# A hybrid attention step on one core: output projection 512 columns wide, sample rows in column tiles of TensorE, and a stricter model behind the order

## The chip, the cores and the metric

One core of one Trainium2 chip runs the whole program. The metric is the device time of one execution in microseconds (us), as the median of several runs. The engines are named as in the profile: PE is TensorE's matmul side, PEld its weight loads, DVE is VectorE, ACT is ScalarE, POOL is GpSimd, SP issues the DMAs.

## The reference, cut to what matters

One layer with three head groups works on 512 prompt rows and 32 sample rows of width 1024. Everything is float32.

```
z = rmsnorm(x) @ w_in                              # q, k, v, gate of A, B, M and the indexer's qi, ki, wi
A: 6 heads x 64, chunk-band attention (own chunk + 8 before), learned relative bias
B: 6 heads x 64, top-k keys by an indexer (8 heads x 32, one key head), rotary
M: 4 heads x 64, cross attention into 256 memory rows (keys, values = rmsnorm(mem) @ w_mem_kv)
x = x + concat(oA*silu(gA), oB*silu(gB), oM*silu(gM)) @ w_out      # w_out is 1024 x 1024
y = rmsnorm(x)                                     # for the prompt and for the sample
```

The sample rows attend to caches (512 rows for A, 1024 for B, 256 for M) and to their own new keys. New keys and values of all groups are outputs too.

## The kernel before, in words

A float32 product with few errors is made of three fp32r products: each operand is split into a high part (`wh`, `xTh`, `oAh`; ACT rounds it) and a low part (`wl`, `xTl`, `oAl`; POOL or DVE subtracts), and PE adds h*h, l*h and h*l. Every weight block goes this way: SP loads `raw`, ACT makes `wh`, POOL makes `wl` (DVE for the block numbers in `WV`). `w_load` and `w_split` do this for one list of blocks, in which the next block waits until a buffer is free.

The order of all instructions is written by a planner at build time. The class `Line` keeps a clock for each engine and a cost for each operation. Work is of two kinds. The main line runs the big projections as quanta (`line.run`); these fill PE. Everything else is a task (a generator) that yields the time at which it may go on: `line.at(x)` is when x should be there, `line.sure(x)` adds a margin `SURE` of 1 us, and costs of all engines but PE are multiplied by `SLACK` (1.3). When a task's time has come by the planner's clock, its instructions go into the queues ahead of the next quantum. `divided` holds an insertion for PE back for at most `HOLD` (3 us) so that two insertions that need tiled modes stand together.

The stages, in PE's order:

- The indexer's projection (`index_group`): row tiles 1, 2, 3 of the prompt want 296 columns, row tile 0 wants the 32 key columns only. DVE and ACT split `x` and the first weights meanwhile. The group starts with clock-warming matmuls on `ident`.
- The projections `EARLY` and `LATE`. The sample rows go through `w_sample`: float32 matmuls on the unsplit `raw`, four k-blocks at a time in four tiles of 32 columns of the array (`tile_position=(0, 32*q)`). Beside them the attention units of A, then M (`attend`: scores, exps, norm, turn, mix, finish).
- Output projection of A and M (`out_part`, first loop): for each 256 columns of `w_out`, five k-blocks (heads A 0 to 2, M 6 and 7), four prompt row tiles in three fp32r products, then the sample as two fp32r products with `oS`, a stationary of 64 columns (high and low parts side by side). This fills PE while the nine units of B and the sample's B attention (`sample_b`) run as tasks. A pair of heads' first scores (`begin`) wait until a score buffer is free, that is until an earlier unit has been transposed (`turn`), and until the pair's q and k are prepared.
- When all units and the sample's B are through: output projection of B (second loop), 512 columns as two parts of 256, sample first, then row tiles 0 to 3; each row tile is added to `xr` by DVE and settled (`settle`: squares on ACT, gain on POOL, the last scale on DVE and ACT, store).

The sample's own attention is `sample(mix, ...)`: scores in column tiles, softmax, transposes of the weights `pt`, and then the mix with values as the stationary (64 columns, two heads side by side) and `pt` as the moving operand (32 columns). The gate product, a rounding and a subtraction make `oS`.

All instructions go through one helper, so the profile puts them on one line, L273, and tiles tell them apart. A float32 matmul appears as two records, an fp32r matmul as one.

Of the kernel before, what the change touches and what calls it, by code (L numbers as in the profile page):

```python
# [17 lines left out]
P = 128  # L18
S = 512
# [15 lines left out]
WV = (0, 2)  # L35
START = "wxwxwxwtwwwwrrrrrmmrr"
SURE = 1.0
SLACK = 1.3
# [7 lines left out]

class Line:
# [4 lines left out]
    def __init__(self):  # L52
        self.clk = dict.fromkeys(("PE", "DVE", "ACT", "POOL", "SP", "DMA"), 0.0)
        self.ready, self.used = {}, {}
# [3 lines left out]
        self.mode = None  # L58
        self.taken = []
# [4 lines left out]
        self.window, self.busy, self.slow = 0.0, 0.0, True  # L64
        self.warm = None

    def cost(self, eng, op, outs, ins, kw):
        if eng == "PE":
# [12 lines left out]
            if mode != self.mode:  # L81
                self.mode = mode
                d += 0.095 + (0.104 if fast else 0.056) * mode[1] / P
            return d
# [6 lines left out]
        if eng == "ACT":  # L91
# [5 lines left out]
            return t  # L97
        return 0.15 + n * (0.0034 if op == "tensor_scalar" else 0.0021)
# [38 lines left out]
    def had(self, x, eng=None):  # L137

        if x.tensor.name not in self.ready:
            return 0.0  # L140
        b = self.box(x)
        return max((t + (self.lag(by, eng) if eng else 0.0) for w, t, by in self.ready.get(x.tensor.name, ())
                    if all(p[0] < q[1] and q[0] < p[1] for p, q in zip(w, b))), default=0.0)

# [21 lines left out]
    def port(self, eng, t, d):  # L166

        for s, end, by in self.taken:
            if by != eng and s <= t < end:
                t = end  # L170
        self.taken = [x for x in self.taken[-40:]] + [(t, t + d, eng)]
        return t

    def op(self, eng, op, outs, ins, kw):
        t = self.clk[eng]
        for x in outs + ins:
            t = max(t, self.had(x, eng))
        if eng == "SP":
            self.clk[eng] = t + 0.05
            t = max(t + 1.6, self.clk["DMA"])  # L180
            end = t + outs[0].size() * 4 / 330e3
            self.clk["DMA"] = end
        else:
            d = self.cost(eng, op, outs, ins, kw) * (1.0 if eng == "PE" else SLACK)
            if eng == "PE":
                d = self.array(t, d)
            elif eng == "POOL" or eng == "DVE" and self.shares(op, outs, ins):
                t = self.port(eng, t, d)
            end = t + d
            self.clk[eng] = end  # L190
        for x in outs:
            if x.tensor.name not in self.ready:
                continue
# [1592 lines left out]
```

## Time and profile before

| | us |
|---|---|
| median of 3 runs | 363.25 (363.15 to 365.74) |
| the profiled execution | 362.68 |
| its span, first to last instruction | 360.6 |
| mean granted clock of TensorE | 0.996 of 2.4 GHz |

The profiled execution is 2.1 us longer than its span, and 0.57 us shorter than the median. PE's busy time is not time at its peak: matmuls are pipelined, so the records of neighbours overlap, and the cost of one in a stream is the distance from its start to the next start.

### The profile page before, as it was taken

To read this page: it belongs to the slowest core of one execution; us is meant where nothing else is said; L and a number is where in the kernel's file an instruction comes from. 1 tells how busy PE (TensorE), PEld (TensorE's weight loads), DVE (VectorE), ACT (ScalarE), POOL (GpSimd) and SP (SyncE) were. 2 spreads that over 40 slices of the span, in tenths; PEclk is the share of its full clock that TensorE was granted. 3 is DMA by queue.
4 is the path that set the end of the run, shared out by engine and by line. 5 is a ranking of instruction groups with operands and counts; after the bars stand their busy time and mean duration, and the time that the engine had idled before them with its cause. 6 is when DMAs were issued, how large, how long until landed. Compare 5 with 4: busy or idle time off the path is not lost.

```text
span 360.6 us, 7941 instructions
## 1 busy us (share of the span) xinstructions
PE 350.7 (97%) x2961; PEld 320.0 (89%) x2961; DVE 276.6 (77%) x696; ACT 219.6 (61%) x521; POOL 191.0 (53%) x213
## 2 busy tenths in 40 slices
PE   8999999999999999999999999999999999999991
PEld 8989988999998989898699898999979878888991
DVE  3665977797888978888999885999868576866463
ACT  5856767896747775595856553217665665544443
POOL 1778983375465574148436464534597412140751
PEclk9999999999999999999999999999999999999998
DMA  7998351475493322531203250133489412000015
GB/s 251 362 362 264 97 176 58 126 202 147 119 293 119 88 52 62 182 90 44 90 3 87 88 166 20 51 108 115 128 294 362 133 45 104 2 2 2 0 40 209
DMA packets 41478, 46.35 MB, mean 129 GB/s; under 512 B 5184, under 2 KB 36544, under 8 KB 41440
## 3 DMA queue, kind: packets, MB, share of 16 engines
q1 hardware_dynamic: 41440, 45.85, 39.9%
q8 instruction: 23, 0.38, 0.4%
q14 instruction: 15, 0.12, 0.1%
HBM read 39.67 MB, written 6.16 MB: 127 GB/s over the span
## 4 chain that ended last, share of the span: by engine, by line
PE 89%; DVE 4%; DMA 2%; issue 1%; ACT 1%; POOL 1%; SPq 1%; POOLq 0%; ACTq 0%; DVEq 0%
PE bank L273 89%; DMA raw<-in_w_in_dram 2%; POOL ss L273 1%; DVE ysel L273 1%; ACT sq L273 1%; DVE xr L273 1%; SPq L273 1%; DVE z L273 1%; DVE m L273 0%; DVE xTl L273 0%; DVE gate L273 0%; ACT wh L273 0%; ACT xTh L273 0%; DVE o L273 0%; DVE pt L273 0%
## 5 line engine op out<-in xcount | busy, mean ns | idle before, releaser
L273 POOL TENSOR_TENSOR wl<-raw,wh 128x512 fp32r<-128x512 f32 (+2 forms) x68 | 110.0, 1622 | 78.2 <-ACT wh L273 74.4
L273 ACT ACTIVATE wh<-raw 128x512 fp32r<-128x512 f32 (+2 forms) x70 | 50.1, 719 | 33.1 <-issue 13.6
L273 PE MATMUL bank<-wh,xTh 128*128 128x384 f32 (+1 forms) x192 | 65.3, 340 | 0.0
L273 PE MATMUL bank<-wl,xTh 128*128 128x384 f32 (+1 forms) x192 | 63.3, 330 | 0.0
L273 PE MATMUL bank<-wh,xTl 128*128 128x384 f32 (+1 forms) x192 | 63.2, 329 | 0.1
L273 ACT ACTIVATE z<-z,st 128x256 f32<-128x256 f32 (+3 forms) x77 | 41.0, 550 | 21.0 <-DVE st L273 20.9
L273 PE MATMUL bank<-xTh,wh 128*128 128x272 f32 x208 | 46.3, 304 | 0.0
L273 PE MATMUL bank<-xTh,wl 128*128 128x272 f32 x208 | 43.0, 288 | 0.0
L273 PE MATMUL bank<-xTl,wh 128*128 128x272 f32 x208 | 43.0, 288 | 0.0
L273 PEld LDWEIGHTS bank<-wh,xTh 128*128 128x128 f32 x192 | 36.1, 188 | 2.3 <-issue 1.6
L273 PEld LDWEIGHTS bank<-wh,xTl 128*128 128x128 f32 x192 | 36.2, 189 | 0.4 <-DVE xTl L273 0.3
L273 PEld LDWEIGHTS bank<-wl,xTh 128*128 128x128 f32 x192 | 36.1, 188 | 0.2 <-POOL wl L273 0.2
L273 PEld LDWEIGHTS bank<-xTh,wh 128*128 128x128 f32 x208 | 32.7, 189 | 1.7 <-issue 0.8
L273 PEld LDWEIGHTS bank<-xTh,wl 128*128 128x128 f32 x208 | 32.6, 189 | 0.1
L273 PEld LDWEIGHTS bank<-xTl,wh 128*128 128x128 f32 x208 | 32.6, 188 | 0.0
L273 DVE MAX8 m<-ysel 128x8 f32<-128x256 f32 (+2 forms) x48 | 26.4, 549 | 0.0
L273 DVE MATCH_REPLACE8 ysel<-m,ysel 128x256 f32<-128x256 f32 (+2 forms) x48 | 26.1, 543 | 0.0
L273 PE MATMUL bank<-ident,z 128*128 128x128 f32 (+1 forms) x161 | 25.0, 273 | 0.0
L273 ACT COPY pt<-bank 128x512 f32<-128x512 f32 (+1 forms) x26 | 14.1, 543 | 14.3 <-PE bank L273 14.2
L273 DVE SCALAR_TENSOR_TENSOR ysel<-r,wI,ysel 128x256 f32<-128x256 f32 (+2 forms) x21 | 17.8, 849 | 6.0 <-ACT r L273 5.6
L273 POOL TENSOR_TENSOR oBl<-o,oBh 128x128 fp32r<-128x128 f32 (+1 forms) x9 | 4.9, 549 | 30.4 <-ACT oBh L273 30.4
L273 PEld LDWEIGHTS bank<-ident,z 128*128 128x128 f32 (+1 forms) x161 | 18.2, 140 | 2.5 <-issue 1.0
(307 smaller groups left out, 892.6 us busy)
## 6 DMA issues: line engine op xcount, KB each, us to landing
raw<-in_w_in_dram SPq DMA_DIRECT2D x20, 384.0 KB, 3.6
raw<-in_w_in_dram SPq DMA_DIRECT2D x26, 256.0 KB, 2.9
raw<-in_w_out_dram SPq DMA_DIRECT2D x8, 384.0 KB, 3.1
nat<-in_x_prompt_dram SPq DMA_DIRECT2D x4, 512.0 KB, 7.9
raw<-in_w_mem_kv_dram SPq DMA_DIRECT2D x8, 256.0 KB, 2.8
xr<-in_x_prompt_dram SPq DMA_DIRECT2D x4, 512.0 KB, 4.8
out_dram<-xr SPq DMA_DIRECT2D x4, 512.0 KB, 2.6
xr<-in_x_t_dram SPq DMA_DIRECT2D x3, 544.0 KB, 5.8
```

The source lines that it names most:

```text
L273: return fn(*args, **kw)
```

## The change

- `w_out` is cut into blocks of one k-block by 512 columns; four k-blocks make a group, AM = (0, 1, 2, 6) and B = (7, 3, 4, 5). The second M block moves behind the attention units, into the group of B. A matmul writes 512 columns; only the last row tile of the last group is cut in two halves.
- The sample leaves `out_part`. `out_sample` multiplies `oS` (float32 now, 32 columns) with the unsplit blocks in four column tiles, 512 columns at once: two pieces for AM and one for B. DVE adds the four quarters to `xrS` one by one. A block's buffer is free for the next load only when its piece has been issued (`met`).
- The sample's mix is turned around: `pt` (32 columns) is the stationary, the values (64 columns) move, four heads in four column tiles. The result is copied to `z`, transposed by PE and multiplied by the gate.
- In `index_group` row tile 0 leaves the loop. `key0` makes its key with eight float32 matmuls in four column tiles and one that adds the quarters and turns them.
- The first weights' `wl` are all made on DVE, the fourth block of `x` has a place of its own, EPS is added on DVE, the sample's rotary goes through PSUM.
- The planner gets operations with dependences (`Op`, `Free`, `When`), replays them in order of time, and `SLACK` is 1.1.
- In `settle` the middle sum moves from DVE to POOL, and the row tile that is finished by DVE alone is the last one, not the one before.
- The sample's B values are loaded once the first half of AM is done. Memory keys and values stay two groups of 256 columns.

```
-WV = (0, 2)
+WV = (0, 1, 2, 3)
-SLACK = 1.3
+SLACK = 1.1
...
+    def op(self, eng, op, outs, ins, kw):
...
+        if share and self.queue["POOL" if eng == "DVE" else "DVE"]:
+            self.last = self.base.copy()
+            self.events()
+        else:
+            self.begin(new, self.start(new))
...
-    for c0 in range(0, D, 256):
-        w_cols(w_out, c0, c0 + 256, 3, 0, 3)
-        w_cols(w_out, c0, c0 + 256, 2, 6, 8)
-    for c0 in range(0, D, 256):
-        w_cols(w_out, c0, c0 + 256, 3, 3, 6)
+    for ks in (AM, B):
+        for c0 in range(0, D, 512):
+            for k in ks:
+                w_cols(w_out, c0, c0 + 512, 1, k, k + 1)
...
-        party = {p + j for _, p, _ in parties for j in range(NK // 2)}
+        party = {p + j for _, p, _ in parties for j in range(NK // 2)} | set(range(n_in, n_in + 16))
...
+    def key0(acc):
+        def issue():
+            p = bank()
+            for j in range(2):
+                for q in range(4):
+                    k = 4 * j + q
+                    PE.matmul(p[q * 32:(q + 1) * 32, 0:P], gw[:, k, :], x_raw[k // 2][:, k % 2, 0:P],
+                              start=(j == 0), stop=(j == 1), tile_position=(0, q * 32))
+            return p
...
+        PE.matmul(acc[:, 256:288], k4, ident4, start=True, stop=True)
+        line.spawn(i_done(0, acc))
...
-            for t in (1, 2, 3, 0):
+            for t in range(1, NT):
...
             def mix_of():
...
+                for pt, b, i, w in blocks:
+                    for j, h in enumerate(hs):
+                        r = where[j]
+                        c = 64 * (h % 2)
...
+                        PE.matmul(o_ps[r * T:(r + 1) * T, g0 * 32 + c:g0 * 32 + c + 64],
+                                  pt[:, i * rows + T * j:i * rows + T * j + T], vv, start=(b == 0),
+                                  stop=(b * P + w == nk), tile_position=(0, r * T))
...
+            PE.transpose(p[:, 0:rows], z[0:rows, 0:P], ident[0:rows, 0:rows])
...
+    def out_sample():
+        yield from line.wait(lambda: count["done"] >= n_am and 2 in over)
...
+        for need, at_, rows in (((0, 2), 0, (0,)), ((0, 2), 4, (512,)), ((1, 2), 8, (0, 512))):
+            i0 = n_in + at_
+            k = 4 * len(rows)
+            yield from line.wait(lambda: len(raws) >= i0 + k and all(m in over for m in need))
+            yield line.sure(oS, *raws[i0:i0 + k])
+
+            def issue():
+                ps = [bank() for _ in rows]
+                for j, p in enumerate(ps):
+                    for q, kt in enumerate(B if at_ == 8 else AM):
+                        PE.matmul(p[q * T:(q + 1) * T, :], oS[:, kt, :], raws[i0 + 4 * j + q][:, 0, :],
+                                  start=True, stop=True, tile_position=(0, q * T))
+                return ps
+
+            ps = yield from divided(len(rows), issue)
+            met.extend(range(i0, i0 + k))
+            line.spawn(out_rows(x, ps, rows))
+
+    def out_rows(xrS, ps, rows):
+        for p, c0 in zip(ps, rows):
+            x = xrS[:, c0:c0 + 512]
+            for q in range(4):
+                yield max(line.at(p, x) - 0.2, line.idle(V))
+                V.tensor_tensor(x, p[q * T:(q + 1) * T, :], x, op=ALU.add)
+            give(p)
...
+        def values():
+            yield from line.wait(lambda: used["done"] >= n_in + 4)
+            cbv.extend((yield from load_cache(("gate0", "q0"), 4, a["cache_b_v"])))
...
+    def out_part(ks, c0, done, order, apart=()):
+
+        ws = []
         for t in order:
...
+                for i, k in enumerate(ks):
+                    if i == len(ws):
+                        ws.append(w_next(1 + i))
+                    wh, wl = (w[:, 0, f0:f0 + n] for w in ws[i])
...
+                    PE.matmul(o, h, wh, start=st, stop=False)
+                    PE.matmul(o, l, wh, start=False, stop=False)
+                    PE.matmul(o, h, wl, start=False, stop=en)
...
+    for c0 in range(0, D, 512):
+        line.run(out_part(AM, c0, lambda *_: None, range(NT)))
     line.until(lambda: 1 in over and count["done"] == len(units))
...
-            V.tensor_scalar(run, new, EPS if j == 0 else old, None, op0=ALU.add)
+            if j == 0:
+                V.tensor_scalar(run, new, EPS, None, op0=ALU.add)
+            else:
+                G.tensor_tensor(run, new, old, op=ALU.add)
...
-        if t == NT - 2:
+        if t == NT - 1:
```

## Rows read from the trace of the kernel before

**Rows 1.** The page: busy time, share of the span and instructions of each engine
```profile
PE 350.7 (97%) x2961; PEld 320.0 (89%) x2961; DVE 276.6 (77%) x696; ACT 219.6 (61%) x521; POOL 191.0 (53%) x213
```

**Rows 2.** Waits of PE over the whole span: us in total, times, longest
```profile
PE bank L273 <- POOL nhalf L273: 1.4, 1, 1.4
PE bank L273 <- ACT pt L273: 0.7, 2, 0.4
```

**Rows 3.** Stretches: us, busy PE, PEld, DVE, ACT, POOL, clock, DMA share, GB/s
```profile
7.18:20.49 13.31, 13.26 (x102) 12.81 (x100) 8.98 (x11) 8.90 (x13) 9.32 (x8) 1.00 1.07 370
266.05:335.01 68.96, 68.96 (x729) 60.66 (x729) 48.65 (x144) 39.36 (x105) 26.29 (x28) 1.00 0.30 105
335.01:352.87 17.86, 17.84 (x158) 17.64 (x156) 10.62 (x20) 8.39 (x22) 10.67 (x12) 1.00 0.11 38
```

**Rows 4.** PE in order of time, output projection: start us, duration us
```profile
272.60 0.28 PE L273 MATMUL bank<-wh,oAh 128*128 128x256 f32 x1
...
273.62 0.28 PE L273 MATMUL bank<-wh,oMh 128*128 128x256 f32 x1
```

**Rows 5.** PE in order of time: the indexer's 512 columns
```profile
89.27 0.39 PE L273 MATMUL bank<-KS,QS 128*128 128x512 f32 x1
89.50 0.41 PE L273 MATMUL bank<-xTh,wh 128*128 128x272 f32 x2
```

**Rows 6.** PE in order of time: ten sample matmuls of the output projection
```profile
276.00 0.28 PE L273 MATMUL bank<-wh,oS 128*64 128x256 f32 x1
...
277.14 0.28 PE L273 MATMUL bank<-wh,oAh 128*128 128x256 f32 x1
```

**Rows 7.** PE in order of time: the sample's B scores, four column tiles
```profile
287.73 1.98 PE L273 MATMUL bank<-keysB,qbS 64*32 64x512 f32 x24
289.64 0.33 PE L273 MATMUL bank<-ident,z 128*128 128x128 f32 x1
```

**Rows 8.** PE in order of time: the sample's mix, two column tiles
```profile
302.36 1.13 PE L273 MATMUL bank<-ptS,cache 128*64 128x32 f32 x32
303.32 0.29 PE L273 MATMUL bank<-keysB,vbS 128*64 128x32 f32 x4
```

**Rows 9.** PE in order of time: three transposes ahead of a quantum
```profile
299.87 0.49 PE L273 MATMUL bank<-ident,z 128*128 128x128 f32 x3
300.12 0.36 PE L273 MATMUL bank<-wh,oMh 128*128 128x256 f32 x1
```

**Rows 10.** PE in order of time: row tile 0 in the indexer's projection, then a wait
```profile
9.95 0.18 PE L273 MATMUL bank<-wh,xTh 128*128 128x32 f32 x1
...
10.54 0.39 PE L273 MATMUL bank<-wh,xTh 128*128 128x296 f32 x1
...
11.58 0.40 PE L273 MATMUL bank<-wh,xTl 128*128 128x296 f32 x1
```

**Rows 11.** DVE in order of time: the last split of x
```profile
14.71 1.65 DVE L273 SCALAR_TENSOR_TENSOR xTl<-xr,g_mix,xTh 128x544 fp32r<-128x544 f32 x1 [0.27 <-ACT xTh L273]
```

**Rows 12.** DVE in order of time: the last two row tiles at the end
```profile
354.57 0.48 DVE L273 TENSOR_SCALAR xr<-xr,ss 128x512 f32<-128x512 f32 x1
354.97 0.21 DVE L273 TENSOR_SCALAR ss<-ss 128x1 f32<-128x1 f32 x1
356.17 0.75 DVE L273 SCALAR_TENSOR_TENSOR xr<-xr,ss,gf 128x512 f32<-128x512 f32 x1 [1.00 <-POOL ss L273]
```

**Rows 13.** DVE, then PE in order of time: the first unit of B, normalized, then transposed
```profile
274.18 1.39 DVE L273 TENSOR_SCALAR z<-z,st 128x128 f32<-128x128 f32 x2
279.86 0.49 PE L273 MATMUL bank<-ident,z 128*128 128x128 f32 x3
```

**Rows 14.** PE in order of time: the third pair's first scores; the last unit's mix
```profile
313.63 0.33 PE L273 MATMUL bank<-k,q 64*128 64x128 f32 x2
331.72 1.94 PE L273 MATMUL bank<-pt,vb 128*64 128x128 f32 x28
```

**Rows 15.** The tile xrS: additions of the sample, ns min/median/max
```profile
L273 DVE TENSOR_TENSOR xrS<-bank,xrS x12: 401/416/682, 277.3 to 345.4; 32x256 f32<-32x256 f32 x8, 32x512 f32<-32x512 f32 x4
```

More of the change, by code (lines that the diff above doesn't have):

```diff
@@ L83, in cost @@
                 d += 0.095 + (0.104 if fast else 0.056) * mode[1] / P
+            elif self.short and fast and op != "transpose" and mode == (P, P):
+                d += 0.084
+            self.short = n <= 64 or op == "transpose" and not fast
             return d
@@ new lines, in start, with begin @@
+    def start(self, o):
+        t = self.last[o.eng]
+        for j, written in o.deps:
+            t = max(t, j.end + (self.lag(j.eng, o.eng) if written else 0.0 if j.eng == o.eng else self.lag(None, o.eng)))
+        if o.share:
+            t = max(t, self.last["DVE port" if o.eng == "POOL" else "POOL port"])
+        return t
+    def begin(self, o, t):
+        last = self.last
+        o.start = t
+        if o.eng == "SP":
+            o.end = max(t + 1.3, last["DMA"]) + o.d
+            o.after = {"SP": t + 0.45, "DMA": o.end}
+        else:
+            d = o.d
+            if o.eng == "PE":
+                (self.window, self.busy, self.slow) = last["array"]
@@ L186, in op @@
                 d = self.array(t, d)
[L187 to L193, printed above, removed]
-            b = self.box(x)
-            w = self.ready[x.tensor.name]
-            w[:] = [e for e in w if not all(q[0] <= p[0] and p[1] <= q[1] for p, q in zip(e[0], b))]
-            w.append((b, end, eng))
@@ L198, in op, with events @@
-        for x in outs + ins:
-            n = x.tensor.name
-            self.used[n] = max(end, self.used.get(n, 0.0))
+            o.end = t + d
+            o.after = {o.eng: o.end}
+            if o.eng == "PE":
+                o.after["array"] = (self.window, self.busy, self.slow)
+            if o.share:
+                o.after[o.eng + " port"] = o.end
+        o.enter(last)
+        self.clk[o.eng] = o.end if o.eng != "SP" else t
+    def events(self):
+        heads = {}
+        at = dict.fromkeys(self.queue, 0)
+        open_ = {o for q in self.queue.values() for o in q}
+        while open_:
+            best = None
+            for eng, q in self.queue.items():
+                if at[eng] == len(q):
+                    continue
+                o = q[at[eng]]
+                if eng not in heads or o.share:
+                    if any(j in open_ for j, _ in o.deps):
+                        continue
+                    heads[eng] = self.start(o)
+                if best is None or heads[eng] < heads[best]:
+                    best = eng
+            o = self.queue[best][at[best]]
+            self.begin(o, heads.pop(best))
+            at[best] += 1
+            open_.remove(o)
@@ L229, in task, with beside @@
             self.push(t, gen)
-    def beside(self, t):
+    def beside(self, when):
         n = 0
-        while self.tasks and self.tasks[0][0] <= max(self.now(), t) and n < 100:
+        while self.tasks and self.tasks[0][0] <= max(self.now(), when()) and n < 100:
             self.task()
@@ L245, in run @@
         for need in quanta:
-            self.beside(max(self.had(x, "PE") for x in need))
+            self.beside(lambda: max(self.had(x, "PE") for x in need))
     def wait(self, cond):
@@ L769, in scale @@
         def scale():
+            yield from line.wait(lambda: count["scored"] > 1)
             for t in range(NT):
@@ L1207, in sample @@
             rows = T * len(hs)
+            if mix == 1 and g0:
+                over["first"] = True
             z = zin(g0, rows)
```

362 lines of the change are left out of this document (246 added, 116 removed).

## Prediction

> **What bounds the kernel now.** I read the page's busy times first: PE's records cover 97% of the span, the next engine, DVE, 77% [rows 1]. Overlapping records could hide a starved PE, so the second view is who waited: PE lost 1.4 us once, before its first matmul, and 0.7 us in two waits for a copy by ACT [rows 2]. The third is the table of stretches: in three stages, the indexer's projection at the start, the stage in which B's attention runs beside the output projection of A and M, and the output projection of B at the end, PE's busy time is all of the stretch or 0.05 us short of it, at a granted clock of 1.00, the level of 2.4 GHz [rows 3]. So PE's queue is the path from 7.2 us to 352.9 us, and what leaves it comes off the time, unless something else becomes late. Distances between starts, not durations, are the prices: nine matmuls of 256 columns go from 272.60 to 273.62, 0.113 us each, although each lasts 0.28 us [rows 4].
>
> **1. The sample leaves the output projection.** Removed are 8 k-blocks x 4 column blocks x 2 products = 64 matmuls of 256 columns. Ten of them take 276.00 to 277.14, 0.114 us each [rows 6]: 7.3 us. Added are four sets of four column tiles, float32, 512 columns. The trace has such sets in the sample's B scores: two of 512 columns, two small ones of 32 and the change of mode take 287.73 to 289.64, 1.91 us [rows 7], so a set costs at most 0.95 us and, without the small ones, some 0.85: 3.4 to 3.8 us, and up to 0.1 us for each of three entries. Net -3.0 to -3.9; I take **-3.5**.
>
> **2. The sample's mix turned around.** There are 92 matmuls, 184 records, before and after. Now 32 records take 302.36 to 303.32, 30 ns each [rows 8]: 5.5 us. Afterwards 64 of the matmuls stand four to a set and 28 in pairs. No row shows sets of 64 columns. From above: 30 ns a record as now, nothing gained. From below: by columns, half a set of 512 in rows 7 is 0.48 us, so 64 columns are 0.06 us for four records, 15 ns each; 128 x 15 + 56 x 30 ns = 3.6 us, 1.9 saved, and a little more is thinkable for the pairs. I take the lower price, since the row is of the same kind of tile. Added are five transposes, one for each group of heads: three take 0.25 us with what follows them 0.1 us late [rows 9], so one costs 0.1 to 0.2 us, 1.0 us at most for five. Net -2.2 to +1.0; I take **-1.0**. DVE and ACT lose a product, a rounding and a subtraction and gain small copies and products, off the path.
>
> The page "TensorEngine Tiling (Array Packing)" of the Trainium skill, section Performance Considerations, speaks against taking a tile factor from a dimension that is already small: each matmul has some 60 cycles whatever its columns. That would be an estimate of 25 ns a record at 2.4 GHz and hardly a gain from the turn; rows 7 neither show nor exclude it at 64 columns.
>
> **3. The start.** Row tile 0 costs 9.95 to 10.54 in each of four k-steps [rows 10], 2.4 us, and PE loses about half a microsecond more between 10.54 and 11.58, where four matmuls take 1.04 us. `key0` puts back two sets of 128 columns (a quarter of 0.95 each), one small matmul and two entries, 0.9 us. The gain is limited by DVE: it works 8.98 of 13.31 us in this stretch [rows 3], ends the last split of x at 16.36 [rows 11] and gets two subtractions more. If that split stays at 16 us, 18 matmuls at 0.15 (9.95 less 7.18, over 18) end at 18.7, not 20.5: 1.8 saved less 0.9. Bounds -2.0 (no wait at all) and -0.2 (DVE later by its two subtractions); I take **-1.0**.
>
> **4. The width.** 384 matmuls at 0.113 us are 43.5 us; 192 of 512 columns take their place. From below: 0.113 is 6.6 ns more than 256 columns at 2.4 GHz, and the same on 512 gives 0.220, 42.2 us. From above: the indexer's 512 columns go from 89.27 to 89.50, 0.23 us [rows 5], 44.2 us. Twelve halves at the end add 0.1. I take 0.224, nearer to rows 4, which are the same loop: **-0.4**, between -1.3 and +0.8.
>
> The page "TensorE: Matmul & The Clock Gate", Part 2, section Back-to-back issue gap, gives N/2.4 + 2.5 ns for a warm matmul. By that estimate 512 columns are 0.216 us, 41.4 us in all, and 256 columns 0.109; rows 4 have 0.113, so I go by rows.
>
> **5. The tail.** The last row tile's sum of squares stands on DVE behind the two last products of the row tile before (354.57 and, after it, 354.97), and its own product starts at 356.17 [rows 12]. With that sum on POOL and the tile before finished by ACT about 1.0 us goes; then the last row tile needs 0.75 + 0.48 us on DVE in series where ACT did half beside it, 0.4 back. **-0.6**, between -1.1 and +0.4.
>
> **6. What the shorter queue may wait for.** This is the open term. The stage from 266.05 to 335.01 holds 68.96 us of PE's work [rows 3]. It loses 240 narrow matmuls (27.2 us) for 96 wide ones (21.5), because the second M block moves behind the stage; it loses 52 of the 64 sample matmuls (5.9) for two or four sets (1.9 to 3.8), and half a microsecond of mix. About 10 us of filler are gone, 3.7 us of them only moved: the last stage grows from 17.86 to 96 x 0.224 + 0.1 = 21.6 us. So sums 1 to 5 hold only if B's nine units and the sample's B get through in some 59 us where they now have 69. For it: the units wait for the planner more than for engines. The first unit's normalized scores are there at 275.57 and PE transposes them at 279.86 [rows 13], 4.3 us later; `SLACK` 1.1 and a true order of the ports bring such places forward, and in the last two microseconds, from 331.72, PE had units alone and did not wait [rows 2, 14]. Against it: DVE has 48.65 us of work there and ACT 39.36 [rows 3]; each pair's q and k are made only after an earlier unit is transposed, and the third pair alone takes from 313.63 to past 331.72 [rows 14]. Bounds 0 and 10 us; I take **+1.0**, near the lower end for rows 13.
>
> Three waits are new and I cost them at nothing. The second half of AM's blocks is loaded after the first sample piece, with SP's queue holding the residual rows and B's keys ahead of it; the first half's 48 matmuls (10.8 us) and B's units lie over that. If that cover is short, PE waits, and it is a part of the 0 to 10 above. The four last blocks are split on ACT and POOL only when B's output projection begins; its first half covers them for 10.8 us, though POOL is busy 10.67 of 17.86 us already, so 1 to 2 us may show. The sample's B values are loaded only when AM's first half is done; its mix is due at 302 at present [rows 8], and the sample alone waits for them, as long as it ends before the units.
>
> **The sum.** -3.5 - 1.0 - 1.0 - 0.4 - 0.6 + 1.0 = -5.5 us against the profiled 362.68: 357.2. That execution is 0.57 us under the median, so 363.25 - 5.5 = **357.8**.
>
> **Rivals.**
> (a) B's chain keeps its length. The stage shrinks by nothing to 4 us (the margin of rows 13 once). Then: start -1.0, tail -0.6, last stage +3.7, stage 0 to -4: 365.4 to 361.4. For it speaks that the filler before seems just enough; against it the margins.
> (b) Slower: B's chain is stretched by DVE. The sample's additions are 8 at 0.41 and 4 at 0.68 us now, 6.0 us [rows 15], and become 16 at 0.68, 10.9. They stand in DVE's queue ahead of B's score reductions and copies. Price up to 4.9 on top of the rigid case, 370.3; it decides from the point at which the stage lasts 1.5 us longer than 68.96 (366.9). Against it: DVE is idle for 20 us of the stage. The Tiling page named above, section PSUM Bottleneck, says that tiles speed up TensorE and not the evacuation; by that rule this is where the gain would go, and rows 15 show that an addition of 512 columns takes 0.68 us for 32 rows only.
> (c) All terms near their good ends and no wait: -3.9 - 2.2 - 2.0 - 1.3 - 1.1 = -10.5, 352.8.
> (d) It does not do what it says: 512 columns cost 0.23, the mix is no cheaper, sets at 0.95 with entries: -3.0 + 1.0 - 1.0 + 0.8 - 0.6 + 1.0 = -1.8, 361.5.
>
> **How the numbers follow.** Forecast (355.5 to 359.6) 0.37, (a) 0.25, (b) 0.08, (c) 0.20 (352 to 355.5), (d) 0.10. A change of 1% (3.6 us) is about what a measurement of this kernel tells from none, so faster is below 359.6 and slower above 366.9. Faster: 0.37 + 0.20 and a little of (a) and (d), 0.60; same: the rest of those, 0.32; slower 0.08. The range leaves out (b) and a little below: 352 to 365.
>
> **What would show it.** Right: the four sets at 0.8 to 0.95 us each, mix records at some 15 ns, starts 0.22 us apart in the output projection, the indexer's stage some 1.8 us shorter, PE still without waits, and B's stage near 59 us. Wrong: waits of PE between the first B scores and the last B mix, or a last stage that waits for `wl`; then (a) or (b) holds, told apart by whether DVE is busy or idle while PE waits.

## The result and the profile after

The changed kernel takes 359.61 us, the median of four runs (358.32 to 360.09), against 363.2 us before on the same chip: a ratio of 0.989 (95% interval 0.987 to 0.991). The profiled execution took 359.21 us, its span is 357.2 us; before, 362.68 and 360.6. So the two profiled executions are 3.5 us apart; in them PE's last matmul ends at 350.03 us instead of 352.85, which is 2.8 us sooner.

The page's busy times:

```profile
PE 346.3 (97%) x2752; PEld 300.8 (84%) x2752; DVE 285.5 (80%) x711; ACT 220.9 (62%) x529; POOL 178.6 (50%) x200
```

PE has 4.4 us less work and the same share of the span as in [rows 1]; DVE has 8.9 us more. PE's waits over the whole span:

```profile
PE bank L397 <- DVE o L397: 1.4, 2, 0.9
PE bank L397 <- POOL nhalf L397: 1.4, 1, 1.4
PE bank L397 <- DVE z L397: 0.6, 1, 0.6
PE bank L397 <- ACT pt L397: 0.2, 1, 0.2
PE bank L397 <- DMA cache<-in_cache_b_v_dram: 0.2, 1, 0.2
```

Against [rows 2] there are 1.7 us more, and the longest of the new waits are for DVE. They stand in the stretch in which the attention units of A run, PE in order of time (start us, duration us):

```profile
133.28 0.18 PE L397 MATMUL bank<-bf_ok,over 128*128 128x1 bf16 x1 [0.92 <-DVE o L397]
139.92 0.39 PE L397 MATMUL bank<-xTh,wh 128*128 128x272 f32 x1 [0.46 <-DVE o L397]
```

DVE is all but full there. From 90 to 185 us it works 90.67 of 95 us, and worked 83.57 in the kernel before (columns as in [rows 3], before and after):

```profile
90.00:185.00 95.00, 94.61 (x861) 84.71 (x860) 83.57 (x260) 65.24 (x164) 50.28 (x54) 1.00 0.36 108
90.00:185.00 95.00, 93.36 (x878) 82.48 (x877) 90.67 (x285) 66.12 (x169) 49.91 (x58) 1.00 0.35 102
```

So 7.1 of DVE's 8.9 us more lie in this stretch. None of the three waits that the prediction feared (blocks of the second half of A and M, the last four splits, the sample's B values) is longer than 0.2 us. The stretches that answer to [rows 3], from the indexer's first matmul to the end of its projection, from B's first scores to B's output projection, and from there to the last matmul:

```profile
8.13:18.39 10.26, 10.26 (x78) 10.09 (x76) 8.31 (x12) 7.97 (x11) 6.11 (x8) 1.00 1.04 338
250.59:326.19 75.60, 74.89 (x663) 57.57 (x662) 58.57 (x155) 45.47 (x120) 29.57 (x33) 1.00 0.41 142
326.19:350.03 23.84, 23.84 (x122) 18.30 (x120) 13.83 (x25) 10.29 (x26) 13.89 (x18) 1.00 0.10 37
```

In the first stretch DVE's last split of x, which the prediction took for the limit, ends at 16.01 us, when the last 18 matmuls (15.85 to 18.39) have just begun; it ended at 16.36 in [rows 11]:

```profile
15.24 0.77 DVE L397 SCALAR_TENSOR_TENSOR xTl<-xr,g_mix,xTh 128x544 fp32r<-128x544 f32 x1
```

The second stretch is the one to look at. The prediction wanted B's units to get through in some 59 us instead of 68.96. The stage is 75.60 us long; what moved is its start, from 266.05 to 250.59. B's first scores and the mix of its last unit, PE in order of time (start us, duration us):

```profile
250.59 0.33 PE L397 MATMUL bank<-k,q 64*128 64x128 f32 x2
...
321.52 1.09 PE L397 MATMUL bank<-pt,vb 128*64 128x128 f32 x16
```

That is 70.9 us from the one to the other; before it was 65.7 ([rows 3] and [rows 14]: 266.05 to 331.72). The chain of B's units grew and ended 10 us sooner all the same. What held its start in the kernel before stood directly ahead of it. These are the last mixes of M's units, before and after:

```profile
265.03 1.09 PE L273 MATMUL bank<-pt,mv 128*64 128x128 f32 x14 [0.37 <-ACT pt L273]
...
235.05 0.82 PE L397 MATMUL bank<-pt,mv 128*64 128x128 f32 x12
```

In the kernel before, B's first scores follow right behind M's last mix. In the changed kernel M's units are through 30 us sooner, and B's first scores stand ahead of the last projections of 272 columns, which go on until 271.4 us.

The wide output projection, PE in order of time, and the four sets of the sample:

```profile
341.26 0.39 PE L397 MATMUL bank<-wl,oBh 128*128 128x512 f32 x1
341.49 0.39 PE L397 MATMUL bank<-wh,oMh 128*128 128x512 f32 x1
341.72 0.39 PE L397 MATMUL bank<-wh,oMl 128*128 128x512 f32 x1
341.95 0.39 PE L397 MATMUL bank<-wl,oMh 128*128 128x512 f32 x1
```

```profile
268.49 1.06 PE L397 MATMUL bank<-raw,oS 128*32 128x512 f32 x8
269.48 0.33 PE L397 MATMUL bank<-ident,z 128*128 128x128 f32 x1
...
330.46 1.92 PE L397 MATMUL bank<-raw,oS 128*32 128x512 f32 x16
332.32 0.50 PE L397 MATMUL bank<-whl,oBh 128*128 128x512 f32 x1
```

Starts of wide matmuls are 0.23 us apart, as the indexer's were in [rows 5], and not the 0.224 of the forecast. A set takes 0.93 to 1.00 us (1.86 for the pair at 330.46), as in [rows 7] or a little more. The sample's mix, which answers to [rows 8]:

```profile
305.74 0.65 PE L397 MATMUL bank<-cache,ptS 128*32 128x64 f32 x32 [0.16 <-DMA cache<-in_cache_b_v_dram]
306.18 0.32 PE L397 MATMUL bank<-vbS,keysB 128*32 128x64 f32 x8
...
323.43 1.09 PE L397 MATMUL bank<-cache,ptS 128*32 128x64 f32 x32
324.35 0.28 PE L397 MATMUL bank<-vbS,keysB 128*32 128x64 f32 x4
325.18 0.27 PE L397 MATMUL bank<-ident,z 64*128 64x64 f32 x1 [0.55 <-DVE z L397]
```

Four to a set, 32 records take 0.44 us, 14 ns each; in pairs 0.92 us, 29 ns each: the prediction's 15 and 30. A pair of 64 columns costs what a pair of 32 cost in [rows 8] (30 ns a record), so the gain comes from standing four to a set. The last row shows what the turned mix brings with it, a transpose that waits 0.55 us for the copy of the result by DVE.

The best account of the 2.8 us on PE is one by kind of work: every matmul of both traces is priced by the distance from its start to the next start, and the prices are added up. A wait of PE is thus in the row of the matmul ahead of it: the 0.92 us above are in the units' mixes, the 0.46 us in the projections of 272 columns.

| kind of work on PE | before, us | after, us | difference |
|---|---|---|---|
| output projection, sample | 8.18 | 3.85 | -4.33 |
| row tile 0's indexer key | 2.42 | 0.60 | -1.82 |
| other row tiles of the indexer | 10.75 | 10.11 | -0.64 |
| fill at the start | 5.96 | 6.92 | +0.96 |
| sample's mix | 5.93 | 5.00 | -0.93 |
| output projection, prompt | 46.36 | 47.49 | +1.13 |
| projections of 272 columns (gates, queries of A and M) | 82.84 | 85.34 | +2.50 |
| projections of 384 columns | 86.67 | 87.08 | +0.41 |
| scores and mixes of the units | 39.05 | 39.58 | +0.53 |
| all the rest (with the five new transposes, +0.58) | 63.33 | 62.71 | -0.62 |

A long stream is interrupted 134 times instead of 114 (counted are its matmuls that take over 0.03 us more than their kind usually does), at about 0.1 us each.

### The profile page after: what moved, and what is told of

Same layout as the page of the kernel before. It is cut to its first block, busy times and chain, and to the rows that moved or that the text cites. A ratio compares the mean times of both kernels' runs of the same rounds, so it can differ in the third digit from the quotient of the medians.

```text
span 357.2 us, 7557 instructions
## 1 busy us (share of the span) xinstructions
PE 346.3 (97%) x2752; PEld 300.8 (84%) x2752; DVE 285.5 (80%) x711; ACT 220.9 (62%) x529; POOL 178.6 (50%) x200
## 4 chain that ended last, share of the span: by engine, by line
PE 80%; DVE 10%; DMA 4%; ACT 3%; issue 1%; POOL 1%; POOLq 0%; SPq 0%; DVEq 0%; ACTq 0%
PE bank L397 80%; DVE ysel L397 2%; DMA cache<-in_cache_b_v_dram 2%; DMA tmpA<-in_bias_s_dram 2%; DVE z L397 1%; DVE gate L397 1%; DVE m L397 1%; ACT junkS L397 1%; DVE xr L397 1%; ACT z L397 1%; DVE tmpA L397 1%; DVE bi L397 1%; DVE pt L397 1%; DVE nb L397 0%; POOL wl L397 0%
## 5 line engine op out<-in xcount | busy, mean ns | idle before, releaser
L397 POOL TENSOR_TENSOR wl<-raw,wh 128x512 fp32r<-128x512 f32 (+1 forms) x69 | 104.0, 1515 | 78.9 <-ACT wh L397 74.2
L397 PE MATMUL bank<-wh,xTh 128*128 128x384 f32 (+1 forms) x184 | 63.2, 343 | 0.0
L397 ACT ACTIVATE z<-z,st 128x256 f32<-128x256 f32 (+3 forms) x81 | 42.5, 548 | 31.4 <-DVE st L397 31.3
L397 PE MATMUL bank<-wl,xTh 128*128 128x384 f32 (+1 forms) x184 | 61.2, 333 | 0.0
L397 PE MATMUL bank<-wh,xTl 128*128 128x384 f32 (+1 forms) x184 | 61.0, 331 | 0.0
L397 PE MATMUL bank<-xTh,wh 128*128 128x272 f32 x208 | 47.7, 309 | 0.7 <-DVE o L397 0.5
L397 PEld LDWEIGHTS bank<-wh,xTh 128*128 128x128 f32 x184 | 34.6, 188 | 1.4 <-issue 0.8
L397 PEld LDWEIGHTS bank<-wh,xTl 128*128 128x128 f32 x184 | 34.7, 189 | 0.1
L397 PEld LDWEIGHTS bank<-wl,xTh 128*128 128x128 f32 x184 | 34.5, 188 | 0.0
L397 PEld LDWEIGHTS bank<-ident,z 128*128 128x128 f32 (+1 forms) x162 | 18.7, 140 | 4.5 <-ACT wh L397 1.1
L397 DVE SCALAR_TENSOR_TENSOR ysel<-r,wI,ysel 128x256 f32<-128x256 f32 (+2 forms) x21 | 18.7, 890 | 4.2 <-ACT r L397 3.9
L397 ACT ACTIVATE junkS<-ysS,bi 128x1056 int8<-128x1056 f32 x16 | 18.7, 1171 | 2.1 <-DVE bi L397 2.1
```

The lines of the kernel that those rows point to most:

```text
L397: return fn(*args, **kw)
```

## The experiments

Each was run beside the kernel before; ratios are to that. The changed kernel's own is 0.989.

**The sample in column tiles.** `e9_sample_rows` takes the sample back into the loop:

```diff
-    oS = cp.tile([P, 8, T], F32, name="oS")
+    oS = cp.tile([P, 8, 2 * T], F32R, name="oS")
+                    if t == NT:
+                        h = oS[:, k, :]
+                        yield (wh, wl, h) + ((acc,) if st else ())
+                        PE.matmul(o[0:2 * T], h, wh, start=st, stop=False)
+                        PE.matmul(o[0:2 * T], h, wl, start=False, stop=en)
+                        continue
```

> The changed kernel with the sample back in the output projection's loop: its result split in high and low fp32r parts side by side, a fifth row tile with two products of 512 columns for each of 8 k-blocks in each of two column blocks (32 matmuls of 512, 7.5 us), two additions for each block; the four sets of column tiles (3.85 us) and their 16 additions go. Theory (PE's queue is the path, term 1 of the prediction is worth what it takes in the trace): 3 to 4 us slower, 362.6 to 363.6. Rival (the stage of B's units ends when its chain ends, as the run with the sets issued twice half suggests): only the last stage's half shows, 1 to 2 us slower.

Measured: 363.82 us, ratio 1.001 (1.000 to 1.002), 4.2 us more than the changed kernel. In its trace the sample's part takes 8.32 us instead of 3.85, and PE's last matmul ends 4.9 us later. Two of its rows, 0.23 us apart like all wide ones although only 64 columns are stationary:

```profile
341.78 0.39 PE L397 MATMUL bank<-wh,oS 128*64 128x512 f32 x1
342.01 0.39 PE L397 MATMUL bank<-wl,oS 128*64 128x512 f32 x1
```

So this one part is worth as much as the whole change: of the 4.9 us, 4.5 are in the sample's own rows, and the other kinds of work come to 0.4 together. The theory held, a little above its upper end. `e3_sets_twice` asked the same from the other side:

```diff
-                    for q, kt in enumerate(B if at_ == 8 else AM):
-                        PE.matmul(p[q * T:(q + 1) * T, :], oS[:, kt, :], raws[i0 + 4 * j + q][:, 0, :],
-                                  start=True, stop=True, tile_position=(0, q * T))
+                    for _ in range(2):
+                        for q, kt in enumerate(B if at_ == 8 else AM):
+                            PE.matmul(p[q * T:(q + 1) * T, :], oS[:, kt, :], raws[i0 + 4 * j + q][:, 0, :],
+                                      start=True, stop=True, tile_position=(0, q * T))
```

> The changed kernel with each of the sample's four sets of column tiles issued twice (the second overwrites the first). In the trace the four sets take 3.85 us. Theory: PE's queue is the path in the stage of B's units too, so the time rises by all of it, 3.5 to 4.0 us, to about 363.4. Rival (the stage of B's units has slack, as the prediction's case a has it): the two sets that stand there cost nothing and only the two in the last stage are seen, 1.7 to 2.1 us.

Measured: 361.35 us, ratio 0.995 (0.994 to 0.996), 1.7 us more than the changed kernel by the medians. Its profile says more: the sets take 7.28 us (+3.43), PE's last matmul ends 3.2 us later, and the profiled execution, 362.11 us, is 2.9 us longer than that of the changed kernel. In it the sample's mix takes 1.0 us less and the transposes of probabilities 0.5 us less, because what they had waited for was there by then; other work takes nearly as much more. So the median is the rival's number and the profile is near the theory's. With runs of the changed kernel from 358.32 to 360.09 us, e3 does not decide between the two by its time; a stage with slack for two sets isn't in its trace, where PE works all of the 80 us from 250 to 330 (79.29 in the changed kernel).

**The margin of the planner.** `e4_margin` and `e10_margin_12` change one constant, to 1.3 (shown) and to 1.2; `e8_before_margin` changes it from 1.3 to 1.1 in the kernel before:

```diff
-SLACK = 1.1
+SLACK = 1.3
```

> The changed kernel with the margin on the planner's costs of DVE, ACT and POOL back at 1.3. In the changed kernel's trace PE waits 0.62, 0.38 and 0.22 us in the gate projections, which it did not before, and the long streams are interrupted 134 times against 114, at about 0.1 us each. Theory: the smaller margin makes both, so with 1.3 the waits go and some interruptions with them: 1.0 to 2.5 us faster. Rival: the units are placed later and B's chain becomes the end of its stage: 1 to 4 us slower. Third: the interruptions come from the number of pieces and not from the margin, within 0.5 us.

Measured: 370.01 us, ratio 1.018 (1.017 to 1.020), 10.4 us slower than with 1.1. The time went the rival's way, at two and a half times its price. The largest waits of PE in it, and B's first scores and last mix:

```profile
PE bank L397 <- ACT z L397: 3.2, 3, 2.2
PE bank L397 <- DVE z L397: 1.6, 1, 1.6
...
PE bank L397 <- POOL wl L397: 1.2, 1, 1.2
PE bank L397 <- ACT pt L397: 1.2, 1, 1.2
```

```profile
263.00 0.33 PE L397 MATMUL bank<-k,q 64*128 64x128 f32 x2
...
332.88 1.09 PE L397 MATMUL bank<-pt,vb 128*64 128x128 f32 x16
```

B starts 12.4 us later than in the changed kernel, directly behind M's last mix again (262.80), and takes as long, 69.9 us. B's output projection starts at 336.65 instead of 326.19, and PE has 11.1 us of waits in the span instead of 3.8. Of these 4.4 us lie behind B's first scores, where the rival has them, and 5.3 between 74 and 256 us, which it did not name.

> The changed kernel with a planner's margin of 1.2, between 1.1 (359.6) and 1.3 (370.0). Theory S (the margin sets how late the units are placed, in proportion): 362 to 367 with B's first scores at 254 to 261 us. Theory C (each margin gives another order and the order decides by chance): anything from 358 to 370, with no relation to where B's first scores stand.

Measured: 359.36 us, ratio 0.989 (0.988 to 0.991), the same as with 1.1. B's first scores stand at 256.00, inside the window that theory S named, and the last mix at 322.22, but the time isn't in S's range: up to here the later start cost nothing. The chain of B's units lasts only 66.2 us here, so it ends as early as with 1.1. DVE works 81.31 us between 90 and 185 us and PE has no wait there at all; the sample's four sets, in other company, cost 1.9 us more. S fell by its time, and C, which allows any time from 358 to 370, is hardly tested by one more point. The start of B goes with M's units: with 1.2 and 1.3, B's first scores follow M's last mix within 0.2 us, as in the kernel before, and with 1.1 M's units are through 15 us ahead of them.

> The kernel before, with nothing of the change but the margin of 1.1 in place of 1.3. Theory (its filler already covers every wait, PE is 97% busy, so earlier units free nothing): within 1 us of 363.2; the units of B start earlier and the projection of A and M goes on behind them. Rival (the margin is worth microseconds by itself, whatever the queue holds): 3 us faster or more. Second rival (only the exact order model can afford the smaller margin): 2 to 6 us slower, with waits of PE for z, pt or o.

Measured: 369.58 us, ratio 1.017 (1.016 to 1.018), 6.2 us slower than the kernel before. The second rival held. Three of PE's waits in it, against 1.4 and 0.7 us in [rows 2]:

```profile
PE bank L273 <- ACT z L273: 2.5, 2, 1.3
PE bank L273 <- POOL wl L273: 1.6, 3, 0.8
...
PE bank L273 <- ACT q L273: 0.9, 1, 0.9
```

B's scores start at 258.56, sooner than before, and its last mix at 325.17; then another 16 us go by until B's output projection starts at 342.2, and the projections of 272 columns have lost 4.9 us to waits and interruptions. DVE works 90.71 us between 90 and 185 us, as in the changed kernel, so it is the margin that packs DVE there. The margin alone is no gain; with the old model of the order it is a loss.

**The smaller parts.** `e5_key_in_loop`:

```diff
-            for t in range(1, NT):
+            for t in (1, 2, 3, 0):
-        line.spawn(key0(acc[0]))
```

> The changed kernel with row tile 0's key back in the indexer's loop (fp32r, 32 columns, four k-steps); the weights times g for the float32 version are not made. In the trace of the changed kernel row tile 0's work takes 0.60 us of PE instead of 2.42, but matmuls that only keep the engine busy take 1.0 us more, and the indexer's stage ends 2.1 us sooner than before. Theory (the stage is PE's queue): 1.2 to 2.1 us slower, 360.8 to 361.7. Rival (the stage ends when DVE's last split of x ends, as the prediction feared): within 0.5 us.

Measured: 358.71 us, ratio 0.988 (0.987 to 0.990), 0.9 us below the changed kernel with intervals that overlap. The theory fell. Row tile 0's key takes 2.42 us of PE again (+1.8), the projections of 384 columns 0.9 us more; but the units' mixes take 1.1 us less, the sample's mix 1.0 and the units' scores 0.4. Most of that is waits: PE's come to 2.0 us here and not 3.8, and the 0.92 us for DVE's `o` are not among them. What row tile 0 saves on PE, the order of the changed kernel gives back in waits. `e6_mix_rows` undoes the turned mix:

```diff
-                        PE.matmul(o_ps[r * T:(r + 1) * T, g0 * 32 + c:g0 * 32 + c + 64],
-                                  pt[:, i * rows + T * j:i * rows + T * j + T], vv, start=(b == 0),
-                                  stop=(b * P + w == nk), tile_position=(0, r * T))
+                            PE.matmul(o_ps[64 * e:64 * e + 64, (h // 2) * T:(h // 2 + 1) * T], vv,
+                                      pt[:, i * rows + T * j:i * rows + T * j + T], start=(b == 0),
+                                      stop=(b * P + w == nk), tile_position=(0, 64 * e))
```

> The changed kernel with the sample's mix as it was (heads in 64 rows, 32 columns of the probabilities as moving operand, pairs of column tiles, products with the gate straight from the bank); the float32 result, the out-projection's sets and all else stay. In the trace the turn took the mix's records from 5.93 to 5.00 us, of which 0.77 is one wait, and added five transposes. Theory (the prediction's value): 1.0 us slower, about 360.6. Rival 1 (a set of four tiles runs together and the transposes are cheap): 1.7 us slower or more. Rival 2 (the copies and transposes eat the gain): within 0.5 us, or faster.

Measured: 358.54 us, ratio 0.987 (0.986 to 0.988). Rival 2 held: the turn brings nothing that can be measured in the time. By the rows the mix takes 5.67 us instead of 5.00 and the five transposes (0.58) go, so little was to be had; PE's waits are 2.6 us and not 3.8. `e11_key_and_mix` undoes both:

> The changed kernel with both the parts undone that were not worth anything by themselves: row tile 0's key in the loop and the sample's mix in rows. Theory (they add up): 0.9 + 1.1 us faster than the changed kernel, about 357.6. Rival (each gave only another order, with waits and interruptions of its own): within 1 us of 359, or slower.

Measured: 364.25 us, ratio 1.003 (1.002 to 1.004), 4.6 us slower than the changed kernel. The theory fell and the rival held. One edit alone looked 0.9 us faster, the other 1.1, the two together are 4.6 us slower. In the trace of the last, the key (+1.8), the sample's mix (+0.8), the sample's four sets, now in other company (+1.7), the projections of 272 columns (+1.0) and the indexer's other row tiles (+0.6) all cost more. So the planner's scatter, some microseconds for any edit that makes it place quanta anew, is larger than these terms, and a run with one part undone can't price them.

`e7_tail_old` does not move a matmul, so it has no such scatter:

```diff
-            if j == 0:
-                V.tensor_scalar(run, new, EPS, None, op0=ALU.add)
-            else:
-                G.tensor_tensor(run, new, old, op=ALU.add)
+            V.tensor_scalar(run, new, EPS if j == 0 else old, None, op0=ALU.add)
-        if t == NT - 1:
+        if t == NT - 2:
```

> The changed kernel with the tail's two edits undone: the running sum of squares on DVE again, and the last row tile's left half finished by ACT, the tile before by DVE. PE's order is the same to the last matmul. Theory: 0.4 to 1.0 us slower, as the last row tile's sum stands on DVE behind the products of the row tile before it again; the span behind PE's last matmul goes from 7.1 to 7.7 us. Rival: nothing, since with the last tile in two halves and 512 columns each the sum comes late enough.

Measured: 360.08 us, ratio 0.991 (0.990 to 0.993), 0.5 us above the changed kernel with intervals that overlap. In its profile PE's last matmul ends at 350.76 (0.7 us were lost in the first 54 us, ahead of anything that the edit touches) and the span 7.3 us behind it, against 7.1. That would make the edits worth 0.15 us, but in the other runs that have them this stretch takes 6.82 to 7.24 us, so 0.15 can't be told from nothing. The DVE sum that stood behind two products in [rows 12] now comes ahead of them, so there was little left to repair. The rest of the shorter tail (7.76 to 7.3) is not the work of these edits; that it came with the new order of the last pieces is argued and not shown.

**The width.** `e1_streams` measures the disputed price by itself.

> Leaves the whole step out: streams of matmuls alone, in the three-product pattern of the output projection, in this order: 96 of 512 columns, 96 of 256, 48 of 512, 48 of 256, 48 of 384, 48 of 256, 48 of 272, 48 of 256, 48 of 512 with zeros as the moving operand, 48 of 512 with zeros in both, then groups of 12 behind four float32 transposes (eight times 256 columns, eight times 512), 48 of 512 from one stationary pair, 48 of 512 beside copies by ACT and additions by DVE and POOL. Theory W (the price belongs to the width): 256 columns start 0.113 us apart in every stretch, 512 columns 0.228 to 0.236, 384 at 0.175, 272 at 0.125. Rival F (fixed part of 6.6 ns, the value that the prediction took; what raised it to 0.233 in the kernel was the work beside it): 512 columns at 0.220 here, and 0.23 or more only in the last stretch. Rival N (the neighbours decide): 256 columns run at 0.118 behind wider ones or behind transposes and at 0.113 after some time, and 512 the same with 0.233 and 0.220. Rival D (the data decide): 512 columns at 0.220 with zeros, 0.233 with the real values.

Measured, PE in order of time, a stretch of 256 columns and one of 512:

```profile
33.08 0.28 PE L70 MATMUL bank<-wl,xh 128*128 128x256 f32 x1
33.20 0.28 PE L68 MATMUL bank<-wh,xh 128*128 128x256 f32 x1
33.31 0.28 PE L69 MATMUL bank<-wh,xl 128*128 128x256 f32 x1
33.44 0.28 PE L70 MATMUL bank<-wl,xh 128*128 128x256 f32 x1
...
47.26 0.39 PE L68 MATMUL bank<-wh,xh 128*128 128x512 f32 x1
47.49 0.39 PE L69 MATMUL bank<-wh,xl 128*128 128x512 f32 x1
47.72 0.39 PE L70 MATMUL bank<-wl,xh 128*128 128x512 f32 x1
```

At a granted clock of 1.00 (2.4 GHz) 256 columns settle at 0.120 us from start to start, 512 at 0.227, 384 at 0.173; 272 take 0.125 on average. Behind a change of width or a transpose, 512 columns first go 0.224 to 0.236 apart for five to nine matmuls. At 512 columns zeros run like data, and copies by ACT and additions by DVE beside the stream change nothing (0.227); POOL's additions had run at the start of the program, so POOL is not tested. So W, F and D fall as they were written; of N only the slow first matmuls are left, for 512 columns. `e2_halves` puts 256 columns into the changed kernel:

```diff
+                for g0 in range(0, n, 256):
+                  o = acc[:, g0:g0 + 256]
-                    wh, wl = (w[:, 0, f0:f0 + n] for w in ws[i])
+                    wh, wl = (w[:, 0, f0 + g0:f0 + g0 + 256] for w in ws[i])
```

> The changed kernel with each matmul of 512 columns of the prompt's output projection as two of 256 into the two halves of the same bank; evictions, loads, splits and the tail stay. 180 wide ones at 0.233 (41.9 us) become 360. Theory W (256 columns at 0.113 wherever they stand): 40.8 us, so 1.1 us faster, about 358.5. Rival F (a fixed part of 6.6 ns for each matmul and some 5% on top that comes from the place): 0.118 each, 42.5 us, 0.5 us slower, about 360.1. Interruptions by B's units cost the same in both; the planner may place them anew, some half a microsecond either way.

Measured: 359.6 us, ratio 0.990 (0.989 to 0.992), no difference. Neither price holds throughout:

```profile
341.36 0.28 PE L397 MATMUL bank<-wh,oMh 128*128 128x256 f32 x1
341.48 0.28 PE L397 MATMUL bank<-wh,oMl 128*128 128x256 f32 x1
341.60 0.28 PE L397 MATMUL bank<-wl,oMh 128*128 128x256 f32 x1
...
342.07 0.28 PE L397 MATMUL bank<-wh,oBh 128*128 128x256 f32 x1
342.18 0.28 PE L397 MATMUL bank<-wh,oBl 128*128 128x256 f32 x1
342.30 0.28 PE L397 MATMUL bank<-wl,oBh 128*128 128x256 f32 x1
```

The upper three are 0.12 us apart, the lower three 0.113, and it goes on so, six and six, through the last stage: 0.116 on average, or 0.232 for 512 columns, what the wide one takes there (0.233). `e12_places` looked for what chooses:

> Leaves the whole step out: stretches of 24 matmuls on zeros in one large tile, a float32 transpose between them, the place of the stationary and of the moving operand varied, then widths. Theory A (the place of the operands decides between 0.113 and 0.120 us for 256 columns): some places run at 0.113 throughout, others at 0.120, in whole stretches. Theory S (the state that a stream falls into is set by how it starts): all places run alike, with the same first few steps. Theory B (the bank or the length of the accumulation decides): only the stretches with 3 or 24 matmuls to a bank differ.

Measured: 256 columns settle at 0.120 us with the moving operand from 512 bytes to 63 KB away, from one or two stationary operands, with 3, 12 or 24 to a bank. Only a shift of the stationary or of the moving operand by 64 or 128 bytes matters (0.118 and 0.119). No place gave the 0.113 of [rows 4] for longer than one matmul, so A holds in a small part and doesn't explain it, S holds for the rest, B falls. The other widths at the end, 240 to 320 columns, run 11 to 13 ns over their columns at 2.4 GHz. What put the loop of before on 0.113 stays open.

## Why the prediction was right, point by point

The forecast was 357.8 us and 359.61 was measured, at the edge of the forecast's own range. The sum came out near because its largest term was right and errors of both signs met in the others, which is in part luck: the terms measure -4.3, -0.4, -1.5, +1.1, -0.6 and +2.2, where -3.5, -1.0, -1.0, -0.4, -0.6 and +1.0 were forecast.

**What bounds the kernel** held in the main: PE is busy for 97% of the span before and after. On the page's chain of work that ended last PE has 80% of the span, where it had 89%, and DVE 10%, where it had 4%; so DVE has become part of the path, between 110 and 139 us above all. What e9 and e4 add on PE (4.9 and 10.5 us at its last matmul) appears in the time (4.2 and 10.4).

**1, the sample (-3.5).** Right, a little small: -4.33 in the account, 4.2 by e9. The sets cost what the scores in [rows 7] said. The 64 removed matmuls cost 8.18 and not 7.3, because ten of them, mostly first or last in a short piece, took 0.17 to 0.26 us each, unlike the ten of [rows 6]. The prediction's own bounds (7.3 less at most 3.8 and 0.3) give -3.2 at the small end and not -3.0.

**2, the mix (-1.0).** The prices were right and the term was not: 14 and 29 ns a record, but the mix saved 0.93 us in all and not 1.9, with a wait of 0.55 us in it, and the five transposes cost 0.58, so -0.35 is left; by e6 without effect on the time. The step to 15 ns "by columns" was in part luck: 64 columns in pairs cost what 32 columns in pairs did, and only the number to a set mattered. The Tiling page of the Trainium skill ("TensorEngine Tiling (Array Packing)", Performance Considerations) put some 60 cycles, an estimate of 25 ns, on every matmul. Here a whole set takes 55 to 57 ns, whether two records of 64 columns stand in it or four, so four side by side do not pay that one after the other.

**3, the start (-1.0).** In the account -1.5, and the indexer's own projection ends at 18.39 instead of 20.48. DVE's two subtractions more did not push its last split of x back: it ended at 16.01, and the projection 2.4 us behind it, much as the prediction had reckoned. (Its 18.7 starts from 16 where its own row has 16.36; the split came out at 16.) By e5 this too has no measurable effect on the time, as the changed kernel has 1.8 us more of waits than e5. Whether 2 and 3 are worth something together, as e11 (4.6 us) would have it, or nothing, as e5 and e6 would, isn't settled.

**4, the width (-0.4).** Here a step failed: "0.113 is 6.6 ns more than 256 columns at 2.4 GHz, and the same on 512 gives 0.220", and with it the choice of 0.224 as "nearer to rows 4, which are the same loop". The 6.6 ns are no fixed part of a matmul: a settled stream has 13.3 ns over its columns at 256, 384 and 512 (e1), and the loop of before happened to run below that. Wide matmuls cost 0.233 in this kernel, a little over the upper bound from [rows 5], and the term is +1.1. e2 shows that the width itself is worth nothing now, either way. By the formula for a single warm matmul on the page "TensorE: Matmul & The Clock Gate" of the Trainium skill, Part 2, Back-to-back issue gap, 512 columns would be an estimate of 0.216 us; the settled stream has 0.227.

**5, the tail (-0.6).** Right in size (7.76 to 7.13 us behind the last matmul) and mostly wrong in cause: the edits named are worth 0.15 us by e7's profile, less than this stretch varies among the runs. That the size came out is luck, as far as the runs show.

**6, what the shorter queue may wait for (+1.0).** Right in direction, too small: +2.2 us are left of the account when terms 1 to 4 are taken out, most of it in the projections of 272 columns (+2.50). The mechanism failed: "sums 1 to 5 hold only if B's nine units and the sample's B get through in some 59 us where they now have 69". They take longer than before. They began 15.5 us sooner, since M's units were through by 236 us, with the last gates as cover. The price is paid ahead of them, in waits for DVE (0.92 and 0.46 us) where the units of A run and in 17 more interruptions of the projections of 272 columns. That the margin and the order model bring the units forward was in the text, as the reason for the lower end; e4 shows the price without the smaller margin, 10.4 us, just above the upper end of 0 to 10, and e8 that the smaller margin needs the changed kernel around it: in the kernel before it costs 6.2 us. The runs don't separate the order model from the other edits.

**The rivals.** (a) did not come in the changed kernel, though its premise did, a chain that keeps its length: e4 is that case, at 370.0 and not 361 to 365, as PE also waited elsewhere. (b) fell as it was written: the sample's additions are 16 of 0.68 us as forecast, and in B's stage, 6.6 us longer, DVE does 9.9 us more (58.57 against 48.65), but PE lost only 0.71 us there. DVE holds PE up all the same, in another place: between 90 and 185 us it is 95% busy, and PE waits 1.4 us for it. With the margin of 1.1 it is as full there in the kernel before (e8), with 1.2 it works 81.31 us and PE does not wait (e10), so the margin and not the sample's additions is behind that. (c) needed the good end of every term; (d) was right about the width (0.233), the sets (0.93 to 1.00) and the small gain of the mix, though not about the price of its records. Its time, 361.5, was as far off as the forecast's.

No run is clearly better than the changed kernel: the two lowest, e6 with 358.54 and e5 with 358.71 us, overlap it in their intervals, and their union is slower.

## What to carry to other kernels

When a stage loses filler, ask not only whether its chain can get shorter but whether it can start sooner on other work; compare the start of the chain in the two traces, and what stood directly ahead of it, before its length. When units are placed earlier, look at the engine that is nearly full where they go. Where a planner writes the order, an edit's price is that of the whole new order: a part of 1 to 2 us can't be priced by undoing it, only by its own rows, and a margin tuned for one version can cost 6 to 10 us in another. A distance between starts that one loop shows is a price of that loop; take another width from rows of that width.

## What the runs showed of the hardware that was not expected

At a granted clock of 1.00 a stream of fp32r matmuls has no single price per width. 256 columns went 0.113 us apart for 18 us in the last stage of before, 0.120 in a settled stream by themselves, and six and six of each in e2, always at the same places of the loop. 384 columns settle at 0.173 and run at 0.175 in the kernel, 512 settle at 0.227 and run at 0.233. At 512 columns neither data nor work by ACT and DVE changed the settled distance; at 256 a shift of an operand by 64 bytes did, by 2 ns. The 0.113 and the 0.120 are 6% apart, and no view of the profile names what chooses between them.

Sets of float32 column tiles with few columns cost alike, whatever stands in them: 60 ns for two records of 32 columns ([rows 8]), 57 for two of 64 and 55 for four of 64.
